# Half-array products in a two-block transformer kernel: which half each product uses, and in which order

## The chip, the core and the metric

The kernel runs on one core of a Trainium2 chip, as one program from inputs in HBM to the output in HBM. The metric is the device time of one execution in microseconds; the median of several runs stands for a kernel. A profile of one execution gives the start and end of every instruction on every engine.

## The reference, cut to what matters

The reference is two transformer blocks on 512 tokens of width 1024, in float32. The change touches attention in both.

```python
# block 1, mixer A: 3 groups of 4 heads, dim 64; windowed attention at dilation 1, 4, 16
s = einsum('bqhd,bkhd->bhqk', q, k) * 64 ** -0.5
s = where(valid, s, -inf); m = max(s); p = exp(s - m); l = sum(p)
o = einsum('bhqk,bkhd->bqhd', p / l, v); lse = m + log(l)
o = sum(softmax(lse over the 3 groups) * o)
# block 1, mixer B: 8 heads, 96 = 64 + 32 rotary for q and k, 64 for v, all 512 keys
s = einsum('qd,kd->qk', q, k) * 96 ** -0.5
o = einsum('qk,kd->qd', softmax(s), v)
mix = (g_a * (o_a @ w_o_a) + g_b * (o_b @ w_o_b)) @ w_out
# block 2, gated linear attention ("hgrn2"): 4 heads, dim 64, chunks of 64 tokens
scores[t, s] = sum_k q[t, k] * k[s, k] * exp(b[t, k] - b[s, k])   # s <= t, b = cumsum(log f)
```

## The kernel before

All matrix products run on TensorE (PE in the profile): a weight load places a stationary operand of up to 128 rows by 128 columns, then a matmul streams the moving operand past it into a PSUM bank of 512 float32 columns. A large projection splits each float32 operand into a rounded high part and a remainder and takes three passes (`mm3`, lines 320 to 322). The small attention products are taken in plain float32, which the compiler turns into two passes, each with a weight load of its own; a transpose takes one. PSUM has eight banks, in three pools: `acc` (4), `mps` (2, for transposes), `ops` (2, for outputs).

Block 1 runs `mix1`, whose attention is `mixers1`. There PE's order is written out by hand (`in_order`); the order on the other engines comes from the scheduler of the framework. A list of items is worked off in a software pipeline: for item n the scores and softmax are issued, then the transpose of the probabilities (`turn`) of an earlier item, then the product with v (`out`) of one earlier still. Between them `fill(k)` issues k steps of other PE work (projections of later heads, gate projections), so that PE has something to do while DVE and ACT compute a softmax.

Mixer A has 16 items (`ItemA`), one for each half `e` of the heads: a head of 64 dimensions lies on partitions 0 to 63 (e = 0) or 64 to 127 (e = 1), so that its q-k product uses 64 of the 128 array rows. An item takes two heads at one (group 0, 192 or 256 keys) or two (groups 1 and 2, 128 keys) token blocks. Each q-k product is followed by a product of the identity with a bf16 mask over the full 128 rows, which adds the mask (lines 970 to 973).

Mixer B has 32 items (`ItemB`): 4 pairs p of heads, 4 query blocks i, 2 heads e of the pair. Scores are 128 queries by 512 keys with a contraction of 96. The softmax is a maximum on DVE (1074), a scaling (1075) and an exponential on ACT with its row sum (1077); the probabilities are not divided by the sum. `turn` transposes them in four pieces (1083). `out` takes the transposed probabilities as stationary operand, 128 columns wide, and 64 columns of v as moving operand (1092), four pieces for each item. After eight items `out` divides by the sums (1097, 1099), transposes the result again (`end`, 1105) and splits it for the projection that follows.

Block 2's gated attention is in `mixers2`. `s256_scores`, `s128_scores`, `s64_scores` and `diag_mm` form score blocks of 256, 128, 64 and, seven times, 64 by 64 tokens (the diagonal blocks and six levels). Each has the loop over the row half e outermost, one `acc` bank for each e; `diag_mm` also alternates `b`, the half of the output partitions, in its innermost loop. DVE or ACT then copies each bank out (1816, 1838, 1861) or merges it under a mask (1881, 1883). `fill(1)` steps stand between these too.

Of the kernel before, what the change touches and what calls it, by code (L numbers as in the profile page):

```python
# [221 lines left out]
def program(ctx: ExitStack, tc: tile.TileContext, A, out):  # L222
# [567 lines left out]
    def mixers1(xs, zs, r_tm, rho, RX, rp, maskb):  # L790
# [152 lines left out]
        class ItemA:  # L943
# [18 lines left out]
            def scores(self):  # L962
                g, j0, e, W, step = self.g, self.j0, self.e, self.W, self.step
                rr = slice(64 * e, 64 * e + 64)
                mo = 256 * min(j0, 1) if g == 0 else 512 + 128 * (g - 1)
                S, self.P = acc(), u("P")
                Sv, Pv = (self.view(x, 1)[:, :, :, 0, 0:W] for x in (S, self.P))
                for jj, j in enumerate(self.js):
                    k0 = self.blocks(j)[0][0]
                    for a in range(2):  # L970
                        PE.matmul(Sv[:, jj, a], lhsT=QKV[g]["q"][a][rr, 128 * j:128 * j + 128],  # L971
                                  rhs=QKV[g]["k"][a][rr, k0:k0 + W], start=True, stop=False)
                        PE.matmul(Sv[:, jj, a], lhsT=identb, rhs=maskb[:, mo:mo + W], start=False, stop=True)
                s = stv[g]
                nm = s[:, j0:j0 + step, e:4:2]
                DVE.tensor_reduce(nm, Sv, axis=AX.X, op=OP.max)
                DVE.tensor_scalar(nm, nm, -0.125, None, op0=OP.mult)
                for jj, j in enumerate(self.js):
                    for a in range(2):
# [80 lines left out]
        OB, rls = [], {}  # L1060

        class ItemB:
# [79 lines left out]
        ends = []  # L1142
        turned = outed = 0
        for n in range(len(items) + 4):
            if n < len(items):
# [6 lines left out]
                items[n].scores()  # L1152
# [7 lines left out]
            todo, ends[:] = ends[:], []  # L1160
            for f in todo:
                f()
# [6 lines left out]
        for f in ends:  # L1169
            f()  # L1170
# [313 lines left out]
    def mixers2(xs, rt, rh, RX, first, s5, p2, pc, wglu, causal, hm, again):  # L1484
# [342 lines left out]
        def s128_scores():  # L1827
            ts = []
            for e in range(2):
                rr = slice(64 * e, 64 * e + 64)  # L1830
                ps = acc()
                for m in range(2):
                    for n in range(2):
                        PE.matmul(ps[:, 256 * m + 128 * n:256 * m + 128 * n + 128],
                                  lhsT=EX[128, m][rr, 256 * n:256 * n + 128],
                                  rhs=EX[128, m][rr, 256 * n + 128:256 * n + 256], start=True, stop=True)
                ts.append(u("s128", tag="h"))
                (ACT.copy if e else DVE.tensor_copy)(ts[e], ps)
# [12 lines left out]
        def s64_scores():  # L1851
            for e in range(2):
                rr = slice(64 * e, 64 * e + 64)
                ps = acc()
                for m in range(2):
                    for j in range(4):
                        PE.matmul(ps[0:64, 256 * m + 64 * j:256 * m + 64 * j + 64],
                                  lhsT=EX[64, m][rr, 128 * j:128 * j + 64],
                                  rhs=EX[64, m][rr, 128 * j + 64:128 * j + 128], start=True, stop=True)
                M2.append(u("s64"))  # L1860
                ACT.copy(M2[e][0:64], ps[0:64])
# [5 lines left out]
        def diag_mm(ops_, mask):  # L1867
            for e in range(2):
                rr = slice(64 * e, 64 * e + 64)
                ps = acc()  # L1870
                for m in range(2):
                    for j in range(4):
                        for b in range(2):
                            c = 128 * j + 64 * b
                            PE.matmul(ps[64 * b:64 * b + 64, 256 * m + 64 * j:256 * m + 64 * j + 64],
                                      lhsT=ops_[m][0][rr, c:c + 64], rhs=ops_[m][1][rr, c:c + 64],
                                      start=True, stop=True)
                mk_ = hm[:, 64 * mask:64 * mask + 64]
# [317 lines left out]
    with phase("m1", u=9, z=12):  # L2196
# [24 lines left out]
```

## Time and profile before

| | |
|---|---|
| median of 3 runs | 1556.38 us (1553.22 to 1557.43) |
| the profiled execution's own time | 1560.49 us, of which the span 1558.8 us |
| PE busy | 1518.4 us, 97% of the span |
| DVE, ACT, POOL busy | 777.1, 584.5, 243.2 us (50%, 37%, 16%) |
| mean granted PE clock | 0.981 |

The span runs from the first to the last instruction of the profile. A PE instruction counts as busy from its start until its result has landed, so consecutive matmuls overlap: what one costs in a stream is the distance between starts, not its duration. The clock column of the stretches is the granted share of the full TensorE clock, 2.4 GHz; its lower level, 1.2 GHz, reads 0.50.

### The profile page before, as it was taken

How to read it: one execution, taken by the hardware profiler on the slowest of the kernel's cores; microseconds unless marked ns; L12 is line 12 of the kernel's file. 1: busy time of each engine (PE TensorE's matmuls, PEld its weight loads, DVE VectorE, ACT ScalarE, POOL GpSimd, SP SyncE). 2: the span in 40 equal slices, each digit the busy share in tenths (PEclk: the TensorE clock that was granted, in tenths of full speed). 3: DMA queues.
4: the chain of work that ended last, by engine and by line, in shares of the span. 5: the costliest groups of instructions: out<-in, count | busy, mean ns of one | idle time of the engine just before them, and what ended most of it. 6: DMA issues, size and time to landing. Idle time of an engine off the chain costs nothing.

```text
span 1558.8 us, 21891 instructions
## 1 busy us (share of the span) xinstructions
PE 1518.4 (97%) x8564; PEld 1281.2 (82%) x8564; DVE 777.1 (50%) x1513; ACT 584.5 (37%) x1099; POOL 243.2 (16%) x513
## 2 busy tenths in 40 slices
PE   8999999999999999999999989989999999999997
PEld 6998987778888888888887889866888888888885
DVE  5423245743556534333545685867637431444346
ACT  6443344533335433324224443433525322322222
POOL 0311201000110275401810032321000000000000
PEclk9999999999999999999999998979999999999999
DMA  8422111112225332323323433101114332332222
GB/s 291 134 82 63 59 46 43 55 41 95 88 80 197 103 95 88 107 77 108 95 83 120 164 109 96 41 28 55 41 55 163 123 101 75 122 95 95 95 95 81
DMA packets 54727, 147.36 MB, mean 95 GB/s; under 512 B 9824, under 2 KB 16368, under 8 KB 54624
## 3 DMA queue, kind: packets, MB, share of 16 engines
q1 hardware_dynamic: 52384, 143.38, 28.2%
q10 hardware_dynamic: 1776, 1.85, 0.4%
q8 instruction: 67, 1.10, 0.3%
q0 software_dynamic: 464, 0.74, 0.2%
q14 instruction: 36, 0.29, 0.1%
HBM read 135.12 MB, written 11.06 MB: 94 GB/s over the span
## 4 chain that ended last, share of the span: by engine, by line
PE 88%; DVE 8%; ACT 2%; DMA 1%; issue 1%; SPq 0%; POOL 0%; DVEq 0%; ACTq 0%
PE acc L320 24%; PE acc L321 24%; PE acc L322 24%; PE acc L1071 2%; PE ops L1092 2%; PE acc L971 1%; DVE wlo L301 1%; PE ops L1013 1%; DVE y L625 1%; PE mps L1083 1%; PE acc L1953 1%; PE ops L320 1%; PE ops L321 1%; PE ops L322 1%; PE ops L1969 1%
## 5 line engine op out<-in xcount | busy, mean ns | idle before, releaser
L300 ACT CAST whi<-wraw 128x1024 fp32r<-128x1024 f32 (+4 forms) x237 | 234.3, 993 | 495.5 <-PE acc L321 239.5
L301 DVE TENSOR_TENSOR wlo<-wraw,whi 128x1024 fp32r<-128x1024 f32 (+4 forms) x237 | 279.6, 1184 | 239.8 <-ACT whi L300 229.9
L320 PE MATMUL acc<-xh,whi 128*128 128x512 f32 (+1 forms) x920 | 349.5, 381 | 7.0 <-ACT whi L300 5.6
L322 PE MATMUL acc<-xh,wlo 128*128 128x512 f32 (+1 forms) x920 | 345.6, 376 | 2.0 <-DVE wlo L301 2.0
L321 PE MATMUL acc<-xl,whi 128*128 128x512 f32 (+1 forms) x920 | 345.9, 376 | 0.3 <-DVE xl L664 0.3
L320 PEld LDWEIGHTS acc<-xh,whi 128*128 128x128 f32 x920 | 175.1, 190 | 44.0 <-ACT whi L300 8.2
L322 PEld LDWEIGHTS acc<-xh,wlo 128*128 128x128 f32 x920 | 175.0, 190 | 34.1 <-DVE wlo L301 2.9
L321 PEld LDWEIGHTS acc<-xl,whi 128*128 128x128 f32 x920 | 175.1, 190 | 31.6 <-issue 1.0
L320 PE MATMUL acc<-whi,hidh 128*128 128x512 f32 x432 | 169.2, 394 | 0.0
L321 PE MATMUL acc<-wlo,hidh 128*128 128x512 f32 x432 | 168.8, 393 | 0.0
L322 PE MATMUL acc<-whi,hidl 128*128 128x512 f32 x432 | 168.5, 393 | 0.0
L320 PE MATMUL acc<-whi,xh 128*128 128x256 f32 (+2 forms) x448 | 134.2, 300 | 0.0
L321 PE MATMUL acc<-wlo,xh 128*128 128x256 f32 (+2 forms) x448 | 131.1, 293 | 0.0
L322 PE MATMUL acc<-whi,xl 128*128 128x256 f32 (+2 forms) x448 | 130.7, 292 | 0.0
L321 PEld LDWEIGHTS acc<-wlo,hidh 128*128 128x128 f32 x432 | 81.3, 188 | 18.1
L320 PEld LDWEIGHTS acc<-whi,hidh 128*128 128x128 f32 x432 | 81.3, 188 | 18.0
L322 PEld LDWEIGHTS acc<-whi,hidl 128*128 128x128 f32 x432 | 81.3, 188 | 18.0
L320 PEld LDWEIGHTS acc<-whi,xh 128*128 128x128 f32 x448 | 89.4, 200 | 1.5 <-issue 1.1
L321 PEld LDWEIGHTS acc<-wlo,xh 128*128 128x128 f32 x448 | 89.4, 199 | 0.1
L322 PEld LDWEIGHTS acc<-whi,xl 128*128 128x128 f32 x448 | 89.3, 199 | 0.0
L1235 POOL TENSOR_TENSOR relu<-relu 128x512 f32<-128x512 f32 (+1 forms) x37 | 36.8, 1002 | 230.8 <-ACT hidh L1234 226.5
L597 DVE TENSOR_TENSOR y<-acc,y 128x512 f32<-128x512 f32 x48 | 33.1, 689 | 63.1 <-PE acc L322 63.0
(533 smaller groups left out, 2216.7 us busy)
## 6 DMA issues: line engine op xcount, KB each, us to landing
wraw<-in_wp_dram SPq DMA_DIRECT2D x211, 512.0 KB, 3.5
hd<-y SPq DMA_DIRECT2D x24, 256.0 KB, 3.2
hr<-hd SPq DMA_DIRECT2D x12, 512.0 KB, 5.3
hr<-in_xt_dram SPq DMA_DIRECT2D x8, 512.0 KB, 5.6
H<-in_xT_dram SPq DMA_DIRECT2D x8, 256.0 KB, 5.2
wraw<-in_wp_dram SPq DMA_DIRECT2D x16, 128.0 KB, 3.8
gain<-in_gv_dram SPq DMA_DIRECT2D x8, 256.0 KB, 4.2
out_dram<-y SPq DMA_DIRECT2D x8, 256.0 KB, 2.1
```

The source lines that it names most:

```text
L300: ACT.copy(hi[:, s], raw[:, s])
L301: eng.tensor_tensor(lo[:, s], raw[:, s], hi.bitcast(F32)[:, s], op=OP.subtract)
L320: PE.matmul(ps, lhsT=w[0], rhs=x[0], start=first, stop=False)
L321: PE.matmul(ps, lhsT=w[0], rhs=x[1], start=False, stop=False)
L322: PE.matmul(ps, lhsT=w[1], rhs=x[0], start=False, stop=last)
L597: DVE.tensor_tensor(y, ps, y, op=OP.add)
L625: DVE.scalar_tensor_tensor(y, y, self.r[:, i:i + 1], self.hs[i][:, 512 * f:512 * f + 512], op0=OP.mult, op1=OP.add)
L971: PE.matmul(Sv[:, jj, a], lhsT=QKV[g]["q"][a][rr, 128 * j:128 * j + 128], rhs=QKV[g]["k"][a][rr, k0:k0 + W], start=True, stop=False)
L1013: PE.matmul(po[:, j % 2, h], lhsT=PTv[0:w, jj, a, b], rhs=QKV[g]["v"][v][0:w, 64 * h:64 * h + 64], start=(b == 0), stop=(b == self.nb - 1))
L1071: PE.matmul(S, lhsT=qT[2 * p + e][0:96, 128 * i:128 * i + 128], rhs=kT[2 * (p % 2) + e][0:96], start=True, stop=True)
L1092: PE.matmul(po[:, 128 * i + 64 * e:128 * i + 64 * e + 64], lhsT=self.PT[:, 128 * kt:128 * kt + 128], rhs=VB[kt][:, 64 * h:64 * h + 64], st ...
L1235: POOL.tensor_tensor(a, a, a, op=OP.mult)
```

## The change

Four edits, and one buffer more in the first stage's pool (`u=9` becomes 10).

**Mixer A.** The mask is added first, by one product over the whole bank, and the q-k products accumulate onto it. The two items e = 0 and e = 1 of one place are scored together, their q-k products in turn: one on rows 0 to 63 into one bank, one on rows 64 to 127 into another. Their softmaxes follow one after the other.

**Mixer B.** The probabilities are divided by their sum before the transpose: a reciprocal of one column and a scaling of 128x512 on DVE for each item. v (64 columns) becomes the stationary operand and the transposed probabilities (128 columns) the moving one; the two heads of a pair are taken together, in turn, one into output partitions 0 to 63, the other into 64 to 127. The output is then already transposed: the reciprocals and scalings of `out` and the transposes of `end` are gone. A product with a zero column opens each of the four output banks.

**Gated attention.** The loop over e becomes the innermost one in all four score functions, so two `acc` banks are held together, and the copies follow after both are done.

```diff
-            def scores(self):
+            def products(self):
...
+                if step == 2:
+                    PE.matmul(S, lhsT=identb, rhs=m.to_broadcast([128, 4, W]), start=True, stop=False)
+                else:
+                    PE.matmul(Sv[:, 0], lhsT=identb, rhs=m.to_broadcast([128, 2, W]), start=True, stop=False)
+                yield
                 for jj, j in enumerate(self.js):
                     k0 = self.blocks(j)[0][0]
                     for a in range(2):
                         PE.matmul(Sv[:, jj, a], lhsT=QKV[g]["q"][a][rr, 128 * j:128 * j + 128],
-                                  rhs=QKV[g]["k"][a][rr, k0:k0 + W], start=True, stop=False)
-                        PE.matmul(Sv[:, jj, a], lhsT=identb, rhs=maskb[:, mo:mo + W], start=False, stop=True)
+                                  rhs=QKV[g]["k"][a][rr, k0:k0 + W], start=False,
+                                  stop=(jj == step - 1 and a == 1))
+                        yield
+
+            def scores(self, other):
+
+                for _ in zip(self.products(), other.products()):
+                    pass
+                self.softmax()
+                other.softmax()
...
-                ACT.activation(self.P, S, AF.Exp, scale=rq[:, i:i + 1], bias=mx,
-                               accum_out=rls[p][:, 2 * i + e:2 * i + e + 1])
+                l = rls[p][:, 2 * i + e:2 * i + e + 1]
+                ACT.activation(self.P, S, AF.Exp, scale=rq[:, i:i + 1], bias=mx, accum_out=l)
+                DVE.reciprocal(l, l)
+                DVE.tensor_scalar(self.P, self.P, l, None, op0=OP.mult)
...
             def out(self):
+
                 p, i, e = self.p, self.i, self.e
-                if i == 0 and e == 0:
+                if e == 0:
+                    last_pt[0] = self.PT
+                    return
+                if i == 0:
                     pos["b", p] = ops()
-                po, h = pos["b", p], 2 * p + e
+                    PE.matmul(pos["b", p], lhsT=identb, rhs=zero.to_broadcast([128, 512]), start=True, stop=False)
+                po = pos["b", p]
                 for kt in range(4):
-                    PE.matmul(po[:, 128 * i + 64 * e:128 * i + 64 * e + 64],
-                              lhsT=self.PT[:, 128 * kt:128 * kt + 128], rhs=VB[kt][:, 64 * h:64 * h + 64],
-                              start=(kt == 0), stop=(kt == 3))
-                if i == 3 and e == 1:
-                    rl, o = rls[p], u("ob")
-                    DVE.reciprocal(rl, rl)
-                    v = lambda x: x.rearrange("p (x d) -> p x d", d=64)
-                    DVE.tensor_tensor(v(o), v(po), rl[:, :, None].to_broadcast([128, 8, 64]), op=OP.mult)
-                    ends.append(lambda: self.end(o))
-
-            def end(self, o):
-                tp = mps()
-                for i in range(4):
-                    PE.transpose(tp[:, 128 * i:128 * i + 128], o[:, 128 * i:128 * i + 128], ident)
-                OB.append(split(tp, nm="ob", tag="h"))
+                    for f, PT in enumerate((last_pt[0], self.PT)):
+                        h = 2 * p + f
+                        PE.matmul(po[64 * f:64 * f + 64, 128 * i:128 * i + 128],
+                                  lhsT=VB[kt][:, 64 * h:64 * h + 64], rhs=PT[:, 128 * kt:128 * kt + 128],
+                                  start=False, stop=(i == 3 and kt == 3))
+                if i == 3:
+                    OB.append(split(po, nm="ob", tag="h"))
...
-                items[n].scores()
+                if n >= 16:
+                    items[n].scores()
+                elif n % 2 == 0:
+                    items[n].scores(items[n + 1])
                 fill(fills[n] if n < 16 else 1 if n % 8 in (1, 3) or n >= 40 and n % 2 else 0)
...
         def s256_scores():
             ts = {}
-            for e in range(2):
-                rr = slice(64 * e, 64 * e + 64)
-                for s in range(2):
-                    ps = acc()
-                    for m in range(2):
-                        PE.matmul(ps[:, 256 * m:256 * m + 256], lhsT=EX[256, m][rr, 128 * s:128 * s + 128],
+            for s in range(2):
+                pss = acc(), acc()
+                for m in range(2):
+                    for e in range(2):
+                        rr = slice(64 * e, 64 * e + 64)
+                        PE.matmul(pss[e][:, 256 * m:256 * m + 256], lhsT=EX[256, m][rr, 128 * s:128 * s + 128],
                                   rhs=EX[256, m][rr, 256:512], start=True, stop=True)
+                for e in range(2):
                     ts[e, s] = u("s256", tag="h")
-                    (ACT.copy if s else DVE.tensor_copy)(ts[e, s], ps)
+                    (ACT.copy if e else DVE.tensor_copy)(ts[e, s], pss[e])
...
         def diag_mm(ops_, mask):
-            for e in range(2):
-                rr = slice(64 * e, 64 * e + 64)
-                ps = acc()
-                for m in range(2):
-                    for j in range(4):
-                        for b in range(2):
+            pss = acc(), acc()
+            for m in range(2):
+                for j in range(4):
+                    for b in range(2):
+                        for e in range(2):
+                            rr = slice(64 * e, 64 * e + 64)
                             c = 128 * j + 64 * b
-                            PE.matmul(ps[64 * b:64 * b + 64, 256 * m + 64 * j:256 * m + 64 * j + 64],
+                            PE.matmul(pss[e][64 * b:64 * b + 64, 256 * m + 64 * j:256 * m + 64 * j + 64],
                                       lhsT=ops_[m][0][rr, c:c + 64], rhs=ops_[m][1][rr, c:c + 64],
                                       start=True, stop=True)
+            for e in range(2):
+                ps = pss[e]
...
-    with phase("m1", u=9, z=12):
+    with phase("m1", u=10, z=12):
```

`s128_scores` and `s64_scores` are changed as `s256_scores` is.

## Rows read from the trace of the kernel before

**Rows 1.** The page: busy time by engine, and the chain that ended last.

```profile
PE 1518.4 (97%) x8564; PEld 1281.2 (82%) x8564; DVE 777.1 (50%) x1513; ACT 584.5 (37%) x1099; POOL 243.2 (16%) x513
...
PE 88%; DVE 8%; ACT 2%; DMA 1%; issue 1%; SPq 0%; POOL 0%; DVEq 0%; ACTq 0%
```

**Rows 2.** Stretches: length, busy us (instructions) of PE, PEld, DVE, ACT, POOL, clock, DMA.

```profile
88.00:250.00 162.00, 161.86 (x1075) 141.26 (x1075) 57.67 (x137) 64.50 (x185) 20.96 (x67) 0.96 0.20 60
250.00:345.00 95.00, 93.93 (x585) 74.77 (x584) 56.86 (x105) 46.16 (x92) 4.82 (x4) 1.00 0.13 42
960.00:1001.00 41.00, 41.00 (x324) 34.34 (x322) 24.49 (x35) 18.50 (x33) 8.12 (x6) 1.00 0.22 69
1001.00:1026.00 25.00, 20.10 (x345) 17.15 (x346) 24.69 (x53) 10.59 (x22) 11.90 (x16) 0.94 0.09 23
```

**Rows 3.** Timeline of PE: begin of three mixer A items, and what follows each.

```profile
95.67 0.59 PE L971 MATMUL acc<-kT,qT 64*128 64x192 f32 x2
...
96.94 0.36 PE L320 MATMUL acc<-whi,xh 128*128 128x256 f32 x1
...
109.96 0.70 PE L971 MATMUL acc<-kT,qT 64*128 64x256 f32 x2
...
111.47 0.38 PE L320 MATMUL acc<-whi,xh 128*128 128x256 f32 x1
...
209.34 0.48 PE L971 MATMUL acc<-kT,qT 64*128 64x128 f32 x2
...
211.53 0.48 PE L320 MATMUL acc<-whi,zh 128*128 128x512 f32 x1
```

**Rows 4.** The chain by time: start, us, what (mixer A's end; mixer B).

```profile
238.33 0.23 PE acc L321
...
306.17 0.84 PE ops L1092 x8
307.01 0.91 PE acc L1071 x2
307.92 0.44 PE mps L1083 x4
```

**Rows 5.** Timeline of the gated attention's score blocks.

```profile
972.19 3.04 PE L1813 MATMUL acc<-hb 64*128 64x256 f32 x16
973.36 0.69 DVE L1816 COPY s<-acc 128x512 f32<-128x512 f32 x1 [1.13 <-PE acc L1813]
...
984.44 1.71 PE L1834 MATMUL acc<-hb 64*128 64x128 f32 x16
...
990.77 1.90 PE L1857 MATMUL acc<-hE 64*64 64x64 f32 x32
...
996.23 1.91 PE L1875 MATMUL acc<-hq,hl 64*64 64x64 f32 x64
```

**Rows 6.** Line 1834 alone, two stretches: busy PE and PEld (instructions in flight), clock.

```profile
984.70:984.80 0.10, 0.10 (x3) 0.10 (x3) 1.00 0.00 0
...
985.30:985.40 0.10, 0.10 (x6) 0.10 (x3) 1.00 0.00 0
```

**Rows 7.** The first and last of four stretches at low clock in mixer A.

```profile
111.60:115.10 3.50, 3.50 (x19) 3.50 (x19) 0.86 (x2) 1.89 (x5) 0.00 (x0) 0.51 0.02 5
...
234.50:238.00 3.50, 3.50 (x10) 2.70 (x9) 0.80 (x2) 2.15 (x9) 0.00 (x0) 0.51 0.03 5
```

**Rows 8.** DVE by line: min/median/max ns of one, first and last start, forms.

```profile
L1097 DVE RECIPROCAL rl<-rl x4: 202/203/203, 261.8 to 338.4; 128x8 f32<-128x8 f32 x4
...
L1636 DVE TENSOR_SCALAR hw<-hf x2: 418/420/422, 900.2 to 900.6; 128x512 f32<-128x512 f32 x2
```

**Rows 9.** Mixer B's two stretches of 6 us with most DVE work.

```profile
276.00:282.00 6.00, 6.00 (x39) 4.75 (x38) 5.39 (x9) 3.29 (x7) 0.00 (x0) 1.00 0.26 89
...
300.00:306.00 6.00, 6.00 (x40) 4.72 (x40) 5.30 (x10) 3.65 (x7) 0.00 (x0) 1.00 0.22 72
```

**Rows 10.** Timeline of the last diagonal products, after a wait.

```profile
1025.77 5.19 PE L1875 MATMUL acc<-hE 64*64 64x64 f32 x96 [3.83 <-DVE cz L1745]
```

More of the change, by code (lines that the diff above doesn't have):

```diff
@@ L960, in view @@
                 return x.rearrange("p (j a b q) -> p j a b q", j=self.step, a=2, b=nb)
-            def scores(self):
-                g, j0, e, W, step = self.g, self.j0, self.e, self.W, self.step
-                rr = slice(64 * e, 64 * e + 64)
+            def products(self):
+                g, j0, W, step = self.g, self.j0, self.W, self.step
+                rr = slice(64 * self.e, 64 * self.e + 64)
                 mo = 256 * min(j0, 1) if g == 0 else 512 + 128 * (g - 1)
                 S, self.P = acc(), u("P")
-                Sv, Pv = (self.view(x, 1)[:, :, :, 0, 0:W] for x in (S, self.P))
+                self.Sv = Sv = self.view(S, 1)[:, :, :, 0, 0:W]
+                m = maskb[:, None, mo:mo + W]
+                if step == 2:
[3 more added lines that the diff above has]
+                yield
                 for jj, j in enumerate(self.js):
@@ L971, in scores, with softmax @@
                         PE.matmul(Sv[:, jj, a], lhsT=QKV[g]["q"][a][rr, 128 * j:128 * j + 128],
-                                  rhs=QKV[g]["k"][a][rr, k0:k0 + W], start=True, stop=False)
-                        PE.matmul(Sv[:, jj, a], lhsT=identb, rhs=maskb[:, mo:mo + W], start=False, stop=True)
+                                  rhs=QKV[g]["k"][a][rr, k0:k0 + W], start=False,
[6 more added lines that the diff above has]
+                other.softmax()
+            def softmax(self):
+                g, j0, e, W, step, Sv = self.g, self.j0, self.e, self.W, self.step, self.Sv
+                Pv = self.view(self.P, 1)[:, :, :, 0, 0:W]
                 s = stv[g]
@@ L1057, in combine_a @@
                 OA.append(split(ps, nm="oa", tag="g"))
-        OB, rls = [], {}
+        OB, rls, last_pt = [], {}, [None]
+        zero = CTX.cp.tile([128, 1], BF16, name="zero")
+        POOL.memset(zero, 0.0)
         class ItemB:
@@ L1141, in mixers1 @@
         fills += [0] * 32
-        ends = []
         turned = outed = 0
@@ L1159, in mixers1 @@
                 turned += 1
-            todo, ends[:] = ends[:], []
-            for f in todo:
-                f()
             while outed < turned and outed <= n - lag - 1:
@@ L1168, in mixers1 @@
         fill(2)
-        for f in ends:
-            f()
         fill.plan.extend(gate(m, "g") for m in order[14:16])
@@ L1828, in s128_scores @@
             ts = []
-            for e in range(2):
-                rr = slice(64 * e, 64 * e + 64)
-                ps = acc()
-                for m in range(2):
-                    for n in range(2):
-                        PE.matmul(ps[:, 256 * m + 128 * n:256 * m + 128 * n + 128],
+            pss = acc(), acc()
+            for m in range(2):
+                for n in range(2):
+                    for e in range(2):
+                        rr = slice(64 * e, 64 * e + 64)
+                        PE.matmul(pss[e][:, 256 * m + 128 * n:256 * m + 128 * n + 128],
                                   lhsT=EX[128, m][rr, 256 * n:256 * n + 128],
                                   rhs=EX[128, m][rr, 256 * n + 128:256 * n + 256], start=True, stop=True)
+            for e in range(2):
                 ts.append(u("s128", tag="h"))
-                (ACT.copy if e else DVE.tensor_copy)(ts[e], ps)
+                (ACT.copy if e else DVE.tensor_copy)(ts[e], pss[e])
             return ts
@@ L1851, in s64_scores @@
         def s64_scores():
[L1852 to L1855, printed above, removed]
-                    for j in range(4):
-                        PE.matmul(ps[0:64, 256 * m + 64 * j:256 * m + 64 * j + 64],
+            pss = acc(), acc()
+            for m in range(2):
+                for j in range(4):
+                    for e in range(2):
+                        rr = slice(64 * e, 64 * e + 64)
+                        PE.matmul(pss[e][0:64, 256 * m + 64 * j:256 * m + 64 * j + 64],
                                   lhsT=EX[64, m][rr, 128 * j:128 * j + 64],
                                   rhs=EX[64, m][rr, 128 * j + 64:128 * j + 128], start=True, stop=True)
+            for e in range(2):
                 M2.append(u("s64"))
-                ACT.copy(M2[e][0:64], ps[0:64])
+                ACT.copy(M2[e][0:64], pss[e][0:64])
         SSd = [u("ssd"), u("ssd")]
@@ L1867, in diag_mm @@
         def diag_mm(ops_, mask):
[L1868 to L1872, printed above, removed]
-                        for b in range(2):
+            pss = acc(), acc()
+            for m in range(2):
+                for j in range(4):
+                    for b in range(2):
+                        for e in range(2):
+                            rr = slice(64 * e, 64 * e + 64)
                             c = 128 * j + 64 * b
-                            PE.matmul(ps[64 * b:64 * b + 64, 256 * m + 64 * j:256 * m + 64 * j + 64],
+                            PE.matmul(pss[e][64 * b:64 * b + 64, 256 * m + 64 * j:256 * m + 64 * j + 64],
                                       lhsT=ops_[m][0][rr, c:c + 64], rhs=ops_[m][1][rr, c:c + 64],
                                       start=True, stop=True)
+            for e in range(2):
+                ps = pss[e]
                 mk_ = hm[:, 64 * mask:64 * mask + 64]
```

## The prediction

> **What bounds the kernel now.** First the page: PE is busy for 97% of the span, and 88% of the chain that ended last is PE [rows 1]. So a microsecond of PE time saved is saved at the end, as long as the other engines keep up where it is saved. The table of stretches shows where they would not [rows 2]. Mixer A (88 to 250 us) leaves PE 0.14 us idle, with DVE and ACT below 40%. Mixer B (250 to 345) leaves it 1.1 us idle with DVE at 60%. Block 2's score blocks lie in two kinds of stretch: up to 1001 us PE is never idle, from there to 1026 DVE is busy for 24.69 of 25.00 us and PE waits. PE time saved there goes back into waiting. Last come the timeline and the chain around each product that is touched [rows 3 to 6, 10], the clock [rows 7] and the DVE operations that come nearest to the added ones [rows 8, 9].
>
> The unit of all that follows is the pass: one weight load with its matmul; a float32 product takes two. A pass that streams 128 columns takes 0.11 us (four in 0.44), one of 512 columns 0.455 (two in 0.91) [rows 4]: about 0.055 us for 64 columns, 0.11 for 128, 0.165 for 192, 0.215 for 256. With 64 moving columns and a 128-column weight load it takes 0.105 (eight in 0.84) [rows 4]: there the load sets the pace.
>
> **Do the halves work side by side?** For column halves the trace says yes. The 64x64 products of line 1857 all use one half of the output and take 1.90 us for 32 passes; those of line 1875 alternate it and take 1.91 for 64 [rows 5], 0.029 a pass for 0.057. For row halves it shows as much where e = 1 follows e = 0 at line 1834: three passes are in flight while one half works, six around the change of halves [rows 6]. Line 1813 agrees: 16 passes of 0.215 would take 3.44 us one after another, and took 3.04 [rows 5]. I take full overlap; the other end, none, is kept for the range.
>
> **Mixer A's scores.** From the first product to what follows them, an item takes 1.27 us with 192 keys, 1.51 with 256 and 2.19 with two blocks [rows 3]. There are four, four and eight: 5.1 + 6.0 + 17.5 = 28.6 us. In the last, each q-k product with its mask takes 2.19/4 = 0.55, where 2 x 0.11 and some 0.06 for a bf16 mask of 128 columns (a quarter of the 0.23 us below) make 0.28; so going over to 64 rows and back costs 0.27 us. Afterwards two items pay it once. A pair has two masks of up to 512 columns, priced by the 0.23 us of one pass of 512 columns of the fast format [rows 4], 0.175 where only 384 are used. Two blocks: 0.46 + 0.27 + 8 x 0.11 (16 passes, two at a time) = 1.61, for 4.38 before: -2.77, four times. 256 keys: 0.46 + 0.27 + 4 x 0.215 = 1.59 for 3.02: -1.43, twice. 192 keys: 0.35 + 0.27 + 4 x 0.165 = 1.28 for 2.54: -1.26, twice. Sum **-16.4**. With no overlap the passes take 6.6 us more: -9.8. The second item's softmax now stands behind the first one's on DVE and ACT, but its transpose comes a round of the loop later, behind at least three fill steps; with both engines below 40% [rows 2] I cost that, and two of four `acc` banks taken at once, at nothing. Were that cover too thin, eight pairs could wait up to a microsecond each.
>
> **The clock in mixer A.** Four stretches of 3.5 us run at a granted 0.51, the 1.2 GHz level; each follows a score item directly (the one at 111.6 us the item that ends at 111.47) [rows 3, 7]. Each costs up to 0.49 x 3.5 = 1.7 us; I take 1.5, as not all of it is streaming. After the change half as many score stretches, each with both halves at work, stand where those stood. The ends are 0 (all four stay) and -6.8; I take **-6.0**.
>
> **Mixer B.** `out` takes 0.84 us for an item, 1.68 for a pair [rows 4]. Afterwards a pair is again 16 passes, of 128 columns, two at a time: 8 x 0.11 + 0.27 for the change of mode = 1.15, so -0.53 sixteen times, -8.5. Four groups of four transposes go (4 x 0.44 = -1.8) and four opening products come (4 x 0.23 = +0.9): -9.4 on PE.
>
> Against it stands DVE. Each of 32 items adds a reciprocal, 0.20 by the nearest row, and a scaling of 128x512, 0.42 [rows 8]: 0.65 with the hand-over, 21 us in all, while four scalings and reciprocals of the results, some 3 us, go. DVE's 56.9 us become about 75 in a stretch of 95 - 9.4 = 86. That fits on average, not everywhere: at 276 and 300 us DVE has 5.39 and 5.30 us of work in 6 [rows 9], and two items more 1.3 there, 6.7 and 6.6, where PE would need 5.4. That makes 2.5 us of waiting. Elsewhere the longer softmax must fit in less: PE now takes 2 x (0.91 + 0.44) + 1.15 = 3.85 us for two items instead of 4.38. Bounds for all waits are 0 and the whole 9.4 and a little more; I take 4, nearer to what the two crowded stretches show. Mixer B: **-5.4**.
>
> Here a rule speaks against the change. In [rows 5] line 1857 takes 0.057 us for a pass of 64 columns, no more than the streaming, so its loads hide behind the matmul before, on the same rows. The Trainium skill, page TensorE: Matmul & The Clock Gate, Part 3 (The mechanism), says that a weight load overlaps running matmuls only if it goes to other rows of the array; the two heads of `out` use all rows. By that a pass of `out` would pay load and stream, 0.057 + 0.11, and mixer B would come out slower. The trace disagrees, and it is a rival of small chance below.
>
> **Gated attention.** `s256_scores`: 8 x 0.215 + 0.27 = 2.0 for 3.04 at best. But one of the four `acc` banks is held by a projection half done, so the fourth score bank waits for the first one's copy, 0.69 us [rows 5]; it ends some 1.85 us in, and 4 x 0.215 + 0.2 follow: -0.1. `s128_scores`: 8 x 0.11 + 0.27 = 1.15 for 1.64 to the next product: -0.5. `s64_scores` and six of the seven `diag_mm` save about 0.9 each, in or before the stretch that DVE bounds [rows 2]: nothing. The last 96 passes start after a wait of 3.83 us at 0.054 a pass, 5.19 in all, twice the 0.029 of line 1875 before [rows 5, 10]; nothing waits for DVE after them at once, and four tiles at work instead of two halve them: -2.5 (0 if passes can't start any closer). Sum **-3.1**, from -6 to +2, because more idle time for PE in the stretch before can also lengthen what runs at 1.2 GHz.
>
> **The sum.** -16.4 - 6.0 - 5.4 - 3.1 = -30.9 us. The profiled execution took 1560.5 us, span 1558.8 and 1.7 around it: it would become 1529.6. It lies 4.1 above the median of the runs shown; against that median the forecast is 1525.5, given as 1526.
>
> **The rivals.**
> - DVE takes all of mixer B's gain. Its instructions run in line: a reciprocal that waits for ACT's row sum holds up the maximum of the next item behind it, and PE the transposes. For it: the crowded stretches [rows 9] and 88% average load. Against it: the scheduler orders DVE by due time, and two items lie between softmax and transpose. Then B gives 0 to +8 instead of -5.4: 1531 to 1539. The Trainium skill's page TensorEngine Tiling (Array Packing), section PSUM Bottleneck, points the same way: packing speeds up PE, not the engines that empty its banks.
> - Row halves overlap less, or mixer A's slow stretches stay: +6.6 or +6.0, 1532 each, 1538 together. For it: the overlap is shown only at a change of halves [rows 6].
> - The weight loads of `out` are not hidden, the page's rule above: 16 x 0.167 + 0.27 = 2.9 for 1.68, +20 in B where -8.5 stood: 1554. The rule and [rows 5] contradict each other.
> - Slower: PE waits in mixer B for each item, and its clock falls as after the wait of 3.83 us [rows 10], from 2.4 to 1.2 GHz. A pass there takes 0.054 us for 0.029; if half of mixer B's 86 us of PE work ran so, that would cost 43 x 0.86 = 37 us: 1563. It decides from 36 us on (31 gained / 0.86). Against it: the clock stood at 1.00 all through mixer B, with PE idle 1.1 us [rows 2].
> - The change doesn't do what it says, since passes of different halves don't start closer together than now: within 3 us of 1556. [Rows 5, 6] speak against it.
>
> **How the numbers follow.** The forecast has a chance of 0.62 (its own range, from the bounds of its terms, 1515 to 1534), DVE 0.14, less overlap or clock 0.13, unhidden loads 0.04, the fallen clock 0.03, no effect 0.04. The first three are faster by more than 0.3%, 4.7 us, about what a measurement of this kernel can tell from no change: 0.89. Unhidden loads and most of no effect lie within: 0.07. Slower: 0.04. The range 1514 to 1542 holds the first three but for their tails.
>
> **What would show it.** In the changed profile a pair of mixer A's items with two blocks should take 1.6 us, `out` of a pair 1.15, with PE's clock at 1.00 through mixer A, DVE in mixer B near 85% and PE idle there by about 4 us more. In block 2 DVE stays full from 1000 us on, with more PE waiting. The prediction is wrong if passes of two halves start 0.11 us apart, or if the chain in mixer B goes through DVE and ACT for most items.

## The result, and the profile after

The change makes the kernel faster by 1.3%: 1536.0 us (median of 4 runs, 1532.85 to 1538.70) for 1556.9 of before in the same session, ratio 0.9867 [0.9846, 0.9889]. The forecast was 1526, range 1514 to 1542. The profiled execution took 1534.06 us, its span 1532.3.

The page first, busy time by engine and the chain that ended last:

```profile
PE 1481.0 (97%) x8516; PEld 1242.9 (81%) x8520; DVE 787.6 (51%) x1569; ACT 583.4 (38%) x1099; POOL 247.5 (16%) x514
...
PE 85%; DVE 9%; ACT 3%; DMA 1%; issue 1%; SPq 0%; POOL 0%; DVEq 0%; ACTq 0%; POOLq 0%
```

PE lost 37.4 us of busy time [rows 1], the span only 26.5: eleven came back as idle time. The stretches show where. They are mixer A, mixer B, block 2's score blocks ahead of the part that DVE bounds, and that part (columns as in [rows 2]):

```profile
88.00:218.00 130.00, 128.65 (x995) 118.07 (x993) 49.31 (x123) 58.12 (x174) 21.86 (x66) 1.00 0.23 67
218.00:321.00 103.00, 98.09 (x625) 68.07 (x629) 76.91 (x175) 51.59 (x104) 5.31 (x5) 1.00 0.14 45
...
936.00:970.00 34.00, 33.65 (x246) 28.39 (x246) 18.02 (x22) 15.11 (x26) 6.99 (x6) 1.00 0.24 67
970.00:1007.00 37.00, 27.04 (x515) 21.69 (x513) 35.89 (x72) 17.48 (x35) 14.06 (x17) 0.82 0.14 44
```

Mixer A ends 21.5 us earlier, at a granted clock of 1.00 for 0.96 [rows 2], and PE is still busy for 128.65 of 130 us. In mixer B PE is idle for 4.9 us, before 1.1 [rows 2], with DVE at 75% on average. From 970 us on DVE is busy for 35.9 of 37 us, PE for 27.0, and the clock averages 0.82, in the same part before 0.89.

PE's timeline shows the touched products: a pair of mixer A's items, two pairs of mixer B's `out`, and the gated blocks.

```profile
141.20 0.59 PE L971 MATMUL acc<-maskb,identb 128*128 128x512 bf16 x2
141.73 1.16 PE L978 MATMUL acc<-kT,qT 64*128 64x128 f32 x16
142.82 0.39 PE L320 MATMUL acc<-whi,xh 128*128 128x256 f32 x1
...
262.45 0.43 PE L1122 MATMUL ops<-PT,vb 128*64 128x128 f32 x2
263.57 1.09 PE L1122 MATMUL ops<-PT,vb 128*64 128x128 f32 x14 [0.69 <-ACT PT L1107]
264.59 1.13 PE L1092 MATMUL acc<-kT,qT 96*128 96x512 f32 x2
...
267.38 0.43 PE L1122 MATMUL ops<-PT,vb 128*64 128x128 f32 x2
268.63 1.09 PE L1122 MATMUL ops<-PT,vb 128*64 128x128 f32 x14 [0.82 <-ACT PT L1107]
...
960.41 1.16 PE L1852 MATMUL acc<-hb 64*128 64x128 f32 x16
...
966.19 1.15 PE L1876 MATMUL acc<-hE 64*64 64x64 f32 x32
...
970.90 1.16 PE L1895 MATMUL acc<-hq,hl 64*64 64x64 f32 x64
...
975.39 0.33 PE L1895 MATMUL acc<-hE 64*64 64x64 f32 x2
977.55 1.16 PE L1895 MATMUL acc<-hE 64*64 64x64 f32 x62 [1.84 <-DVE ssd L1903]
...
1003.42 3.57 PE L1895 MATMUL acc<-hE 64*64 64x64 f32 x126 [5.00 <-DVE cz L1762]
```

The pair of items with two blocks takes 142.82 - 141.20 = 1.62 us, where 1.61 was forecast. The blocks of 128 and 64 tokens and a `diag_mm` that doesn't wait take 1.15, for 1.71, 1.90 and 1.91 [rows 5]. But `out`, in 6 of its 16 pairs, and `diag_mm` now stop after two passes and wait.

Two questions are open: which of the gains is due to halves that work side by side, and where the PE time of mixer B and of the diagonal products went. For them whole times are less telling than stages, read from PE's timeline: mixer A from its first score to mixer B's first; mixer B from there to the end of its last product, or of the transposes of `end` where there are any; the diagonal products from first to last; gated attention from the first block of 256 tokens to the end of its output products. All in us. Times are medians, stages are read from the one execution that was profiled; where nothing in a stage was edited, mixer B scatters by 0.6 us, gated attention by less than 1. The before of the three single runs took 1553.6.

| kernel | mixer A | mixer B | diagonal | gated | time | ratio |
|---|---|---|---|---|---|---|
| before | 151.4 | 105.6 | 34.7 | 72.8 | 1556.9 | |
| changed | 129.7 | 102.5 | 36.1 | 73.5 | 1536.0 | 0.9867 [0.9846, 0.9889] |
| A alone | 129.8 | 105.6 | 34.2 | 72.4 | 1537.1 | 0.9869 [0.9833, 0.9905] |
| B alone | 150.7 | 103.4 | 34.5 | 72.7 | 1554.7 | 0.9983 [0.9963, 1.0003] |
| gated alone | 147.7 | 105.7 | 37.7 | 75.6 | 1562.2 | 1.0029 [1.0010, 1.0048] |
| no division | 129.7 | 100.4 | 35.6 | 71.4 | 1531.7 | 0.9831 [0.9801, 0.9862] |
| A in sequence | 138.2 | 105.5 | 34.2 | 72.3 | 1542.0, one run | |
| A masks first | 131.8 | 105.1 | 34.7 | 72.9 | 1537.3, one run | |
| B heads apart | 129.7 | 106.0 | 37.7 | 79.7 | 1542.0, one run | |
| A and B | 129.7 | 102.1 | 34.6 | 72.7 | 1532.3 | 0.9848 [0.9833, 0.9863] |
| all but diag_mm | 129.7 | 102.6 | 33.2 | 70.1 | 1532.8 | 0.9842 [0.9829, 0.9855] |
| diag_mm alone | 148.5 | 105.7 | 35.3 | 74.3 | 1560.2 | 1.0015 [1.0004, 1.0026] |
| scaling on POOL | 129.7 | 101.9 | 37.7 | 78.0 | 1541.0 | 0.9890 [0.9875, 0.9905] |
| `out` later | 129.7 | 99.0 | 35.3 | 72.2 | 1527.5 | 0.9825 [0.9800, 0.9851] |

### The profile page after: what moved, and what is told of

It reads as the page before. It is cut to its first block, busy times and chain, and to the rows that moved or that the text cites. A ratio compares the mean times of both kernels' runs of the same rounds, so it can differ in the third digit from the quotient of the medians.

```text
span 1532.3 us, 21856 instructions
## 1 busy us (share of the span) xinstructions
PE 1481.0 (97%) x8516; PEld 1242.9 (81%) x8520; DVE 787.6 (51%) x1569; ACT 583.4 (38%) x1099; POOL 247.5 (16%) x514
## 4 chain that ended last, share of the span: by engine, by line
PE 85%; DVE 9%; ACT 3%; DMA 1%; issue 1%; SPq 0%; POOL 0%; DVEq 0%; ACTq 0%; POOLq 0%
PE acc L320 24%; PE acc L322 24%; PE acc L321 24%; DVE wlo L301 1%; PE acc L1092 1%; PE ops L1032 1%; PE ops L1122 1%; DVE y L625 1%; PE ops L322 1%; PE ops L320 1%; PE ops L321 1%; PE acc L1975 1%; ACT whi L300 1%; PE ops L1991 1%; PE acc L978 1%
```

## Experiments: the parts alone

The first three keep one part of the change each; all else is as before, but for the tenth buffer of the first stage's pool, which every run here has (`out` later has eleven). No run has the buffer alone. A alone keeps the part that begins with

```diff
+            def products(self):
...
+            def scores(self, other):
```

> Mixer A's edit alone. My theory (denser products and no low clock in mixer A carry the change): mixer A's stretch, from its first score to mixer B's first, falls from 151.4 to about 130 us, as in the changed kernel, no stretch at 1.2 GHz in it, and the time falls by 20 to 22 us. Rival (the three edits share the gain): the time falls by 10 to 14 us. Mixer B and the gated attention take as long as before.

B alone keeps the division ahead of the transpose and the new `out`:

```diff
+                DVE.reciprocal(l, l)
+                DVE.tensor_scalar(self.P, self.P, l, None, op0=OP.mult)
...
+                if e == 0:
+                    last_pt[0] = self.PT
+                    return
```

> Mixer B's edit alone. My theory (DVE takes back most of what PE saves): mixer B, from its first score to the last product before the split, falls from 105.6 to 102 to 103 us, and the time by 2 to 4 us. Rival (mixer B pays in full, its wait in the changed kernel came from the faster mixer A before it): 96 us, and the time falls by 9 us.

Gated alone keeps e as the innermost loop of all four score functions:

```diff
+            pss = acc(), acc()
...
+                        for e in range(2):
+                            rr = slice(64 * e, 64 * e + 64)
```

> The gated attention's edit alone. My theory (DVE bounds the stretch, so passes that start closer only wait longer): from the first score block to the end of the output products 72.8 us before, 72 to 74 after, the time within 2 us of before. Rival (the forecast's step: the last diagonal products are saved): 70 us, the time 3 us lower.

A alone gives the whole gain, as expected. B alone gives 2.2 us in its stage (103.4, just above the 102 to 103 expected), and a time whose interval just reaches no change. Gated attention alone missed both expectations: it is slower by 0.3%, its stage takes 75.6 us and its diagonal products are 3.0 us longer. The buffer doesn't make them longer: A alone and B alone have it too, at 34.2 and 34.5.

## Experiments: what the halves do in mixer A

A in sequence is A alone without the alternation: mask and products of e = 0, then mask and products of e = 1.

```diff
-                for _ in zip(self.products(), other.products()):
-                    pass
+                for x in (self, other):
+                    for _ in x.products():
+                        pass
```

> Mixer A's edit alone, but the two row halves are not alternated: all of e = 0 (its mask, then its products), then all of e = 1. Read from the stage from the first score of mixer A to the first of mixer B, 129.8 us with the edit alone and 151.4 in the kernel before. Theory 1 (the gain is two halves at work side by side, plus masks merged into one product): without alternation the 64-row passes run one after the other and some 6.6 us come back, less what the queue overlaps at the one change of halves; the stage takes 134 to 137 us and a pair with two blocks 2.4 us for 1.62. Theory 2 (the gain is the merged mask and the fewer changes between 64 and 128 rows, the halves do not matter): 129 to 131 us, a pair 1.6 to 1.9 us.

A masks first puts both masks ahead, then the products of e = 0, then those of e = 1.

```diff
-                for _ in zip(self.products(), other.products()):
-                    pass
+                ps = self.products(), other.products()
+                for p in ps:
+                    next(p)
+                for p in ps:
+                    for _ in p:
+                        pass
```

> Mixer A's edit alone, with both masks first, then all q-k products of e = 0, then all of e = 1: two changes of mode for a pair as in the edit, but no alternation. Against the run in sequence it takes out one change between 64 and 128 rows for each pair, 0.27 us by the prediction, eight times: 2 us less than that run, so 132 to 135 us for the stage if the halves matter (a pair with two blocks 2.1 us for 1.62), 129 to 130 if they do not. If a change of rows costs nothing, it is equal to the run in sequence.

In sequence the stage is 8.4 us longer, more than expected, as the expectation left out the second change of rows; the prediction's two terms (6.6 for no overlap, 8 x 0.27 for that change) make 8.8. The full-row mask between the halves keeps them apart. PE's timeline of that run, one pair with two blocks:

```profile
145.02 1.19 PE L978 MATMUL acc<-kT,qT 64*128 64x128 f32 x8
146.14 0.39 PE L971 MATMUL acc<-maskb,identb 128*128 128x512 bf16 x1
146.46 1.16 PE L978 MATMUL acc<-kT,qT 64*128 64x128 f32 x8
147.54 0.39 PE L320 MATMUL acc<-whi,xh 128*128 128x256 f32 x1
```

Eight passes of one half take 1.12 and 1.08 us, as long as sixteen of both in the changed kernel (1.09). Theory 1 holds: in the changed kernel the halves work side by side.

But the halves need not alternate. With the masks first the stage is only 2.0 us longer than with the edit, far from the 8.4 and just under the 132 to 135 us expected. The timeline of that pair, and the instructions of its products in flight in four stretches (columns: PE, PEld, clock, DMA share, GB/s):

```profile
142.01 1.71 PE L978 MATMUL acc<-kT,qT 64*128 64x128 f32 x16
143.65 0.38 PE L320 MATMUL acc<-whi,xh 128*128 128x256 f32 x1
```

```profile
142.10:142.20 0.10, 0.10 (x1) 0.10 (x2) 1.00 1.02 358
142.40:142.50 0.10, 0.10 (x3) 0.10 (x3) 1.00 0.09 21
142.70:142.80 0.10, 0.10 (x6) 0.10 (x6) 1.00 0.00 0
143.20:143.30 0.10, 0.10 (x3) 0.10 (x2) 1.00 0.00 0
```

The eight passes of e = 0 stand ahead of the eight of e = 1 in the program, and yet the products take 1.64 us where one after another would take 2.2. One to three are in flight, then six, then three. By the starts, four passes come alone (142.009 to 142.446); with the fifth, at 142.558, another begins at 142.563, and two such pairs follow (142.777 and 142.781, 142.888 and 142.893); the last five are alone again. The records don't name the half; it is read from passes that start together, which passes on one half never do. The first pass of e = 1 thus starts with the fifth of e = 0, four passes ahead of its place. With only four passes for each half (192 or 256 keys) nothing is lost: a pair with 256 keys takes 1.60 us with the masks first, 1.59 alternating. Alternating is worth 0.55 us for a pair with eight passes each, 2.2 us over the four such pairs, the 2.0 that the stage shows.

The clock needs a correction too. All ten profiled executions with the new mixer A, the one in sequence among them, stay at 1.00 throughout it; the four with the old one have one to four stretches at the 1.2 GHz level, though three of them have the tenth buffer. So the edit does remove them, but two halves at work at once are not needed for it: in the one execution in sequence they never are. Whether the fewer and shorter score stretches or the merged masks do it, no run here settles.

## Experiments: where mixer B's gain went

No division takes the reciprocal and the scaling of the probabilities out of the changed kernel, so its mixer B leaves out the division by the row sum.

```diff
-                DVE.reciprocal(l, l)
-                DVE.tensor_scalar(self.P, self.P, l, None, op0=OP.mult)
```

> All edits, but mixer B's probabilities are not divided by their sums: the reciprocal and the scaling of each of the 32 items are left out, and with them 21 us of DVE work. If that work is what mixer B's PE waits for, mixer B falls from 102.5 to about 96 us and the time by 5 to 7 us against the changed kernel (some 27 us against before). Rival (the longer mode changes and loads of the 64-column products take the gain): mixer B stays at 102 us.

Scaling on POOL moves only the scaling:

```diff
-                DVE.tensor_scalar(self.P, self.P, l, None, op0=OP.mult)
+                POOL.tensor_scalar(self.P, self.P, l, None, op0=OP.mult)
```

> The whole change, but the scaling of mixer B's probabilities by the reciprocal of their sum is done by POOL, which is idle in mixer B, and not by DVE. The nearest rows on POOL with 128x512 take 1.07 to 1.4 us for DVE's 0.49. Theory 1 (DVE's load costs mixer B its 2 us against the run without the division): mixer B 100.4 to 101.5 us for 102.5, the time 1.5 to 2 us less than the whole change. Theory 2 (it is the delay from exponential to transpose, not the load): POOL's longer step makes mixer B 103 to 108 us.

B heads apart takes the four pieces of one head, then those of the other:

```diff
-                for kt in range(4):
-                    for f, PT in enumerate((last_pt[0], self.PT)):
+                for f, PT in enumerate((last_pt[0], self.PT)):
+                    for kt in range(4):
```

> The whole change, but the product with v takes the four pieces of the pair's first head and then the four of the second, so that passes into the two column halves do not alternate. If the halves work side by side only when they alternate, a pair's product takes 16 x 0.11 + 0.27 = 2.0 us for 1.02 to 1.41, and mixer B, 102.5 us with the change, takes 102.5 + 16 x 0.85 = 116 at most, less where PE waited anyway: 110 to 116. If PE's time in mixer B is given back to waiting for DVE and ACT (the rival), mixer B stays within 102 to 106. If column halves bring nothing in this product, a pair keeps its 1.0 to 1.4.

Without the division mixer B takes 100.4 us: the DVE work costs it 2.1 us, where some 6 were expected, so that work is not what holds most of the gain back. On POOL the scaling takes 1.58 us and 0.6 of the 2.1 come back; mixer B's 101.9 us lie between the two theories, nearer to the first. In both runs the waits of `out` stay (2.7 us without the division, 0.7 with POOL) or go over to the transposes (3.8 us with POOL). Heads apart, a pair's product takes 1.51 us for 1.0 to 1.2 without waits, less than the 2.0 expected, since the second head's first pass starts with the first head's fifth (252.542 and 252.536), as in mixer A:

```profile
252.05 1.58 PE L1122 MATMUL ops<-PT,vb 128*64 128x128 f32 x16
```

Mixer B comes out 3.5 us longer, at 106.0, for 16 products that are longer by 0.49 each, 7.8 in all: PE's waits for the copy fall from 3.0 to 0.2 us. The waits that PE has in mixer B of the changed kernel, and ACT's timeline around one of them:

```profile
PE ops L1122 <- ACT PT L1107: 3.0, 6, 0.8
PE mps L1106 <- DVE P L1101: 1.1, 3, 0.4
```

```profile
263.41 0.78 ACT L1099 ACTIVATE P<-acc,mxb,rq 128x512 f32<-128x512 f32 x1
264.09 0.20 ACT L1099 ACTIVATION_READ_ACCUMULATOR P<-acc,mxb,rq 128x1 f32 x1
267.23 0.78 ACT L1099 ACTIVATE P<-acc,mxb,rq 128x512 f32<-128x512 f32 x1 [2.95 <-DVE mxb L1096]
267.91 0.19 ACT L1099 ACTIVATION_READ_ACCUMULATOR P<-acc,mxb,rq 128x1 f32 x1
268.00 0.57 ACT L1107 COPY PT<-mps 128x512 f32<-128x512 f32 x1
```

This is the wait of 0.82 us at 268.63. ACT copies the second head's transposed probabilities only after an exponential, for which it has idled 2.95 us: the scaled maximum it needs is late on DVE, where a copy of line 927 (0.42 us) stands between the maximum and its scaling. DVE itself is not full; over mixer B it idles 8.1 us in front of the reciprocal, waiting for ACT's row sum:

```profile
L1101 DVE TENSOR_SCALAR P<-P,rl 128x512 f32<-128x512 f32 x32 | 15.4, 483 | 0.5
...
L1100 DVE RECIPROCAL rl<-rl 128x1 f32<-128x1 f32 x32 | 5.1, 161 | 8.4 <-ACT P L1099 8.1
```

The two engines wait for each other in line, and PE's product comes too early for both. If that is so, a later product needs no less DVE work. The last run tests it, on all but diag_mm:

```diff
-            while outed < turned and outed <= n - lag - 1:
+            while outed < turned and outed <= n - lag - 1 - (outed >= 16):
...
-    with phase("m1", u=10, z=12):
+    with phase("m1", u=11, z=12):
```

> The edits of mixers A and B and of the blocks of 256, 128 and 64 tokens, diag_mm as before (1532.8 us with mixer B 102.6), and the product of a pair with v one item of the loop later, with one buffer more in the pool u (11). Theory 1 (mixer B's missing gain is the order of ACT: the copy of the second head's transposed probabilities stands behind an exponential that waits for DVE, and the pair's product starts before it): the 3.0 us of PE's waits for that copy go, and mixer B takes 99 to 100 us, the time 1528 to 1531. Theory 2 (DVE and ACT together set the pace, and a wait taken from one place comes back at another): the wait moves to the transposes (L1106) or the scores, mixer B stays within 101.5 to 103, the time within 1531 to 1535.

Mixer B takes 99.0 us for 102.6. The kernel's 1527.5 us are the lowest median of all, though the intervals of the two ratios overlap; the stage is what tells. PE's timeline of two pairs, and what PE waits for there:

```profile
261.65 0.63 PE L1106 MATMUL mps<-cstt,P 128*128 128x128 f32 x4 [0.80 <-DVE mxb L1096]
262.42 1.09 PE L1122 MATMUL ops<-PT,vb 128*64 128x128 f32 x16
263.44 1.13 PE L1092 MATMUL acc<-kT,qT 96*128 96x512 f32 x2
...
266.24 1.09 PE L1122 MATMUL ops<-PT,vb 128*64 128x128 f32 x16
267.26 1.13 PE L1092 MATMUL acc<-kT,qT 96*128 96x512 f32 x2
```

```profile
PE mps L1106 <- DVE mxb L1096: 3.7, 3, 2.1
...
PE mps L1106 <- DVE P L1101: 0.4, 1, 0.4
```

The product takes 1.02 us and waits no more for the copy. Theory 1's sizes hold, the time half a microsecond below them. Part of theory 2 is there too: 3.7 us of waiting moved to the transposes. The longest of these waits, 2.12 us up to 234.12, is followed by 3.4 us at a granted clock of 0.50, the 1.2 GHz level, in which one pair's product takes 1.91 us; so the 99.0 hold a slow stretch that the 102.6 don't. What the eleventh buffer does by itself, no run shows.

## Experiments: what gated attention costs

A and B is the changed kernel with all four functions as before; all but diag_mm has only that one as before:

```diff
         def diag_mm(ops_, mask):
-            pss = acc(), acc()
...
+            for e in range(2):
+                rr = slice(64 * e, 64 * e + 64)
+                ps = acc()
```

> The edits of mixers A and B, gated attention as before. Theory 1 (the gated edit costs a few microseconds because the stretch is bounded by DVE and PE only waits more): faster than the whole change by 1 to 4 us, 1532 to 1535. Theory 2 (gated attention is neutral, and the 4.6 us of its run alone were a chance order of other work): as the whole change, 1535 to 1537.

> As the run of mixers A and B, with the edits of the score blocks of 256, 128 and 64 tokens as well, but diag_mm as before. The blocks of 128 and 64 tokens are 0.55 and 0.74 us shorter; the first lies where PE sets the pace, the second ahead of the stretch that DVE bounds. Theory 1: up to 1 us faster than A and B alone, 1531 to 1534. If instead the blocks of 256 to 64 tokens are what costs: slower than A and B alone by 2 us or more.

The third is the reverse, the kernel before with the new `diag_mm` and, as all runs here, the tenth buffer.

> Only diag_mm's edit, on the kernel before. Theory 1 (it is diag_mm that costs, as it takes two score banks at once in a stretch where DVE frees them late): slower by 3 to 5 us, as the gated edit alone (1.0029): 1.002 to 1.003, and the stretch of the diagonal products 36 to 38 us for 34.7. Theory 2 (diag_mm is neutral and the cost comes with the other three): 1.000.

With gated attention left as it was the time is 1532.3 for 1536.0, as theory 1 said, though the intervals of the two ratios overlap; that its edit costs time is clear from gated alone. The blocks of 256 to 64 tokens make no difference that these runs can tell (1532.8 with them, 1532.3 without); `diag_mm`, with the tenth buffer, costs 0.15% [0.04, 0.26], 2.3 us. That is less than theory 1 had (1.002 to 1.003, and 35.3 us for its 36 to 38) and more than nothing. Over all kernels of the table the diagonal products average 36.7 us with its edit (six, 35.3 to 37.7) and 34.4 without (eight, 33.2 to 35.3). PE's timeline of two calls, with the edit (diag_mm alone) and without (all but diag_mm):

```profile
997.99 0.32 PE L1875 MATMUL acc<-hE 64*64 64x64 f32 x2
999.84 1.16 PE L1875 MATMUL acc<-hE 64*64 64x64 f32 x62 [1.53 <-DVE ssd L1883]
...
1025.86 3.35 PE L1875 MATMUL acc<-hE 64*64 64x64 f32 x126 [5.83 <-DVE cz L1745]
```

```profile
975.25 1.15 PE L1895 MATMUL acc<-hE 64*64 64x64 f32 x32
977.11 1.15 PE L1895 MATMUL acc<-hE 64*64 64x64 f32 x32 [0.71 <-DVE ssd L1901]
```

With e outermost, a call does half of its passes in the first bank before it needs the second, and DVE can merge the first while PE fills the second. With e innermost the second pass needs the second bank already: two passes, a wait, then 62. PE's waits in this stretch are 8.7 us with the edit (5.8, 1.5 and 1.4) for 4.9 in the kernel before (3.8 and 1.1); the passes themselves are faster by 0.75 us a call, which DVE's pace makes worthless.

One thing limits these comparisons. The order on DVE is worked out anew for each kernel, and an edit in mixer B can move it in block 2. In heads apart and scaling on POOL the last four merges of `diag_mm` stand together behind line 1768, where in the changed kernel two stand ahead of it. There the first projection after the diagonal products waits 2.8 and 2.3 us for them, in the changed kernel 0.5, and gated attention takes 79.7 and 78.0 us. Their whole times, 1542 and 1541, hold that shift and say nothing against their mixer B.

## Why the prediction was right, and where its terms were off

The largest term, mixer A, held part by part, and it alone carries the change. Mixer B brought less than forecast and gated attention cost time: 1536 lies in the stated range, but above the forecast's own, 1515 to 1534, and inside that of the rival that gives mixer B's gain to DVE, 1531 to 1539.

**Mixer A, -22.4 forecast, -21.7 measured.** The pairs came out at 1.62, 1.59 and 1.27 us, forecast 1.61, 1.59 and 1.28, so the -16.4 stands, and with it the full overlap of row halves and the 0.27 us for a change of rows. The clock is left with 5.3, forecast 6.0. Of the reason given for it, both halves at work fell; half as many score stretches was not tested. That its size fits is in part luck: it hung on the execution profiled. [Rows 7] holds four slow stretches, three later executions with the old mixer A (and the tenth buffer) one or two, one of these twice as long, and their stages are 147.7 to 150.7 us. Against the mean of the four, 149.6, the edit is worth 19.8.

**Mixer B, -5.4 forecast, -3.1 measured.** The mis-sized term is the waiting, priced at 4. From its start to the start of what follows, `out` of a pair takes 1.78 us before on average, 1.47 in the changed kernel and 1.07 where it is one item later. Free of waits the product would have brought 16 x 0.71 = 11.4 us, for the 8.5 forecast (a pair takes 1.02 where 1.15 was said, so 0.27 for the change of mode was too much here). The transposes (-1.7) were as said, the opening products took 4 x 0.31 = 1.2 for 0.9. Of these 11.8 the stage shows 3.1, so some 8.7 were lost where 4 were forecast. PE's idle time grew by 3.8 only, from 1.1 to 4.9, about what the prediction named as a sign: a stop costs more than its idle time, since PE counts as busy until results on the way have landed. The pair at 262.45 waits 0.69 us and takes 2.14, 1.12 more than one that doesn't wait. The prediction looked for the waiting in DVE's load at two crowded places; DVE came to 75%, not 85%: 76.5 us of work in 102.5, where the prediction had 75 in 86 and left out mixer B's first ten us. Of the 8.7, 16 x 0.40 = 6.4 us are `out` standing too soon behind a copy that is late on ACT: one item later they are gone from `out`, and 3.6 of them reach the stage. The rest is not separated.

**Gated attention, -3.1 forecast, +0.7 in the profile.** The blocks of 128 tokens gave 0.55 for 0.5, those of 256 nothing for 0.1, those of 64 nothing in the end, as forecast. The step that failed is the -2.5 for the last 96 passes: it took the wait ahead of them as given. The passes did become faster (126 in 3.57 us for 96 in 5.19 [rows 10]), but the wait for DVE grew from 3.83 to 5.00, and other calls wait as well. Two of four `acc` banks taken at once, which the prediction priced at nothing in mixer A and not at all here, are harmless there and cost time here. The prediction's sentence for the upper end, more idle PE time and then a lower clock, came true: 0.82 for 0.89.

**The sum.** Of the 10 us between the forecast's -30.9 and the medians' -20.9, mixer A makes 0.7, its scatter 1.9, mixer B 2.3, gated attention 3.8; the other 1.3 lie within the runs' spread.

**The rivals.** DVE as mixer B's limit holds half: the reciprocal waiting in line is in the trace (8.1 us), yet mixer B is still 3.1 us shorter. The chain goes through DVE and ACT for some 30 of its 102.5 us, before for 6 of 105.6: not for most items, which was to be the sign of a wrong prediction, but far more than before. In the diagonal products, what the Trainium skill says on its page TensorEngine Tiling (Array Packing), section PSUM Bottleneck, agrees with the trace: packed passes fill banks faster than DVE empties them, at 35.9 of 37 us. The unhidden weight loads fell: heads apart still runs single passes of 128 columns 0.11 us apart with the loads on the same rows, against the rule of the Trainium skill's page TensorE: Matmul & The Clock Gate, Part 3 (The mechanism); the same section also lets loads go ahead into a background weight buffer, which this trace would fit. In the changed kernel no clock fell in mixer B, and passes of two halves do start together.

## What to carry to other kernels

Products that use half of the array gain when two halves stand next to each other with nothing of full width between them; with four passes for each half it didn't matter here which order they stand in. Before packing them, look at what empties their banks: taking two banks at once where that engine is full trades PE time for waiting, and here cost about 2 us (0.6 to 4). Where a faster product catches up with a copy, one step more of distance in the pipeline can give back more than a lighter load on the late engine: 3.6 us of the stage here, for 2.1 with the division left out altogether.

## What the hardware showed beyond the expected

A matmul on one half of the array starts before matmuls on the other half that stand ahead of it in the program: four passes ahead with row halves (masks first) and with column halves (heads apart). The Trainium skill's page TensorE: Matmul & The Clock Gate, Part 3 (The mechanism), says that matmuls start and end strictly in program order; for the starts, across halves, these traces disagree (a profile's ends are modelled and settle nothing). The kernel before shows it too, unnoticed in the prediction: in the block of 256 tokens [rows 5] the first pass of e = 1, ninth in the program, starts with the fifth (973.163 and 973.156). Part of the overlap that the change writes out was there before.
